# Hybrid decoder step with routed experts: the blocks of four experts moved behind the ranked pairs, and three edits ahead of them

## The chip, the cores and the metric

One core of a Trainium2 chip runs the whole step. The metric is the device time of one execution in microseconds (us); the median of three runs stands against the median of three runs of the changed kernel. One further execution was recorded by the profiler, and all rows below come from it.

## What is computed

A decoder layer is run on 288 tokens: 256 of a prompt and 32 of eight short samples. D is 2048, all in 32-bit floats.

```python
h  = rmsnorm(x, norm_mix)
y, conv, state = mixer(h)             # w_in, convolution + HGRN2 recurrence, w_out
x  = x + y
h2 = rmsnorm(x, norm_ffn)
ids, w = two_level_top2(h2)           # 4 groups of 8 experts; two experts per token
for e in range(32):                   # w_gate, w_up: 2048 x 512; w_down: 512 x 2048
    x += w[e] * (silu(h2 @ w_gate[e]) * (h2 @ w_up[e])) @ w_down[e]
out = rmsnorm(x, norm_final)
# outputs: the 288 rows, the new convolution buffers, the new recurrent states
```

The weights of an expert are 12.6 MB, those of all 32 are 403 MB, and each is read from HBM once.

## The kernel before

The kernel has one body, `trunk_step`. A planner orders each engine's instructions by priority on a simulated time line of its own; at run time every engine then takes its list strictly in order, and waits by semaphores. `tc.issue_after(i)` puts the instructions of its block that are on the engine of `i` behind `i` in that engine's list; it holds back no other engine.

**Front** (lines 250 to 336). `load_x` brings x in two halves. Seven short vectors are brought by GpSimd's queue into `prow`, transposed (line 280) and copied by ScalarE into `par` (line 281). The 16 column blocks of x are transposed by `xpose` (lines 291 to 294), eight per half of x. VectorE multiplies each with `par` and the norm's factor into `hT`, tiles `ha` and `hb` (line 316). The first two projections read `hT` and the raw weights (line 194); from the third on, `project` splits each weight tile on ScalarE into `hi` (line 201) and on VectorE into `lo` (line 202) and makes three matmuls per block (lines 205 to 207).

**Mixer and output projection** (to line 930). The mixer's columns follow, then 16 columns of `w_out`, with `raw`, `hi` and `lo` as weight slots. The recurrent states of sample heads 4 to 7 are finished here: `late_loads` (line 876) is called at column 2 and loads four 512 KB tiles into three of the five `xb` slots and scales them on VectorE behind each load (line 881); `late_state` (line 888) makes the update by four matmuls per head and half on TensorE, copies it on ScalarE and stores it by GpSimd's queue. Heads 4 and 5 are done behind the last column (line 930), heads 6 and 7 within the first pair of experts. Six of the first pair's gate tiles are loaded ahead (`load_ahead`).

**Routing** (lines 944 to 1050). VectorE computes the choice of experts; ScalarE makes `h2` in six pieces (line 963). `keys`, `weights` and `ids` compute the remaining places, the weights of the slots and the ranks of the later experts.

**Experts** (from line 1167). A `Block` has 128 rows: two experts of 64 rows, or four of 32. `gather` q (four quarters) brings the tokens by one-hot matmuls into `xg` (line 1180); `gu(vi, q)` makes a quarter of the gate (vi 0) or up (vi 1) product; `hidden` makes silu(gate) times up (lines 1209 and 1210), so its ScalarE instruction marks the time at which the gate product is done; `turn`, `down`, `out` and `combine` follow. All its matmuls go through `mm`, line 1062, in program order. The weights come in 1 MB tiles, 24 of them for a pair and 48 for a block of four, through a ring of 16 slots (`xa`, `xb`, `raw`, `hi`, `lo`) on SyncE's queue (line 867); a tile is asked for once its slot is free. `in_a_row` runs blocks so that the next block's gather lies beside the present one's down product. The last block ends in `last_down`, which takes the down weights by four column chunks (`wlast`, line 854), the last two of them in halves, and finishes the output norm.

The order of the blocks is: eight pairs of experts 0 to 15; then a block of four; a branch for overflow tiles, ahead of which ten tiles of the next block are loaded (`MIDPRE`); a second block of four; and four pairs. The four pairs hold the eight fullest of the experts 16 to 31, the blocks of four the eight others, by ranks computed on the chip and read into SyncE's registers (`static_id`).

## Time and profile before

| | us |
|---|---|
| median of three runs (lowest, highest) | 1599.75 (1597.68, 1601.33) |
| the profiled execution, its own time | 1599.1 |
| its span on the core | 1596.6 |
| TensorE busy (its granted clock, mean) | 1468.3 (0.971) |
| VectorE, ScalarE, GpSimd busy | 644.8, 448.2, 31.9 |
| moved by DMA | 492.78 MB |

Times in the rows are microseconds from the span's start. "L1062" is line 1062 of the kernel; behind `[` stands how long the engine had been idle ahead of the instruction, and what released it. A granted clock of 1.00 is 2.4 GHz, 0.50 is 1.2 GHz. Because `mm` is one helper, all expert matmuls have line 1062 and are told apart by their tiles: `tp` gather, `att` gate and up, `o` down, `z` combine.

### The profile page before, as it was taken

The page shows a single profiled execution, that of the slowest core. Times are in us where ns is not written, and L with a number is a line of the kernel's source. Part 1 is how long each engine was busy: PE and PEld are TensorE (multiplying, and loading weights), DVE is VectorE, ACT ScalarE, POOL GpSimd, SP SyncE. Part 2 cuts the span into 40 slices and gives each one's busy share as a digit, 9 for nine tenths or more (in the row PEclk, how much of TensorE's full clock was granted, in tenths as well). Part 3 has the DMA queues.
Part 4 walks back from the last instruction along what each step waited for, and adds up shares of the span by engine and source line. Part 5 has one row for each costly group of instructions (what it writes and reads, how often), then busy time and mean ns, then how long its engine had stood idle before and what let it go on. Part 6 is the DMA issues. An engine that isn't in the chain of part 4 may idle for free. (4 is left out here: it accounts for less than half of the span.)

```text
span 1596.6 us, 22199 instructions
## 1 busy us (share of the span) xinstructions
PE 1468.3 (92%) x8898; PEld 918.8 (58%) x8898; DVE 644.8 (40%) x1317; ACT 448.2 (28%) x968; POOL 31.9 (2%) x53
## 2 busy tenths in 40 slices
PE   5999999999979979999999999999666788999995
PEld 3999998999879954543544544544114242543531
DVE  4567788887554443223223223123013022313214
ACT  4467775985834451000000000000000000000013
POOL 1000001000000000000000000000000000000000
PEclk9999999999989989999999999999887899999998
DMA  9645446545498547999999999999998999999992
GB/s 218 172 117 155 138 140 189 159 137 135 111 255 253 156 158 287 396 408 416 419 411 417 419 414 417 419 415 420 418 408 359 421 406 421 415 415 421 415 405 94
DMA packets 228310, 492.78 MB, mean 309 GB/s; under 512 B 13593, under 2 KB 157545, under 8 KB 194936
## 3 DMA queue, kind: packets, MB, share of 16 engines
q1 hardware_dynamic: 225448, 485.09, 81.6%
q0 software_dynamic: 2608, 6.13, 1.2%
q8 instruction: 72, 1.18, 0.3%
q14 instruction: 38, 0.31, 0.1%
q10 hardware_dynamic: 144, 0.07, 0.0%
HBM read 483.92 MB, written 8.18 MB: 308 GB/s over the span
## 5 line engine op out<-in xcount | busy, mean ns | idle before, releaser
L1062 PE MATMUL att<-xb,xg 128*64 128x512 f32 (+1 forms) x640 | 175.2, 634 | 11.9 <-DMA xb<-in_w_exp_up_dram 9.6
L1062 PEld LDWEIGHTS tp<-P,h 96*128 96x128 f32 x1344 | 158.3, 196 | 42.8 <-issue 24.0
L1062 PE MATMUL tp<-P,h 96*128 96x128 f32 x1344 | 166.9, 283 | 15.1 <-DVE P L1169 8.6
L202 DVE TENSOR_TENSOR lo<-raw,hi 128x1024 fp32r<-128x1024 f32 x124 | 147.7, 1222 | 51.4 <-ACT hi L201 51.2
L201 ACT CAST hi<-raw 128x1024 fp32r<-128x1024 f32 x124 | 123.8, 1049 | 88.0 <-PE z L206 59.2
L1210 DVE TENSOR_TENSOR hid<-hid,att 128x512 f32<-128x512 f32 x14 | 9.6, 688 | 311.8 <-PE att L1062 311.8
L1062 PE MATMUL att<-raw,xg 128*64 128x512 f32 (+1 forms) x384 | 119.8, 617 | 8.5 <-DMA raw<-in_w_exp_up_dram 7.0
L1234 ACT ACTIVATE yh<-o,wc 128x512 fp32r<-128x512 f32 x56 | 38.5, 687 | 306.8 <-PE o L1062 287.5
L1062 PE MATMUL att<-xa,xg 128*64 128x512 f32 (+1 forms) x512 | 106.9, 618 | 10.2 <-DVE xg L1180 6.6
L1245 DVE TENSOR_TENSOR acc<-acc,z 96x512 f32<-96x512 f32 x104 | 66.6, 680 | 118.2 <-PE z L1062 118.0
L205 PE MATMUL z<-hhb,hi 128*128 128x288 f32 x368 | 112.0, 304 | 0.0
L206 PE MATMUL z<-hla,hi 128*128 128x288 f32 x368 | 110.9, 301 | 0.0
L207 PE MATMUL z<-hhb,lo 128*128 128x288 f32 x368 | 110.9, 301 | 0.0
L206 PE MATMUL z<-hlb,hi 128*128 128x288 f32 x368 | 110.6, 301 | 0.0
L205 PE MATMUL z<-hha,hi 128*128 128x288 f32 x368 | 110.2, 300 | 0.0
L207 PE MATMUL z<-hha,lo 128*128 128x288 f32 x368 | 109.8, 298 | 0.0
L1062 PE MATMUL att<-lo,xg 128*64 128x512 f32 (+1 forms) x256 | 101.2, 620 | 2.9 <-DMA lo<-in_w_exp_up_dram 2.9
L1235 DVE SCALAR_TENSOR_TENSOR yl<-o,wc,yh 128x512 fp32r<-128x512 f32 x56 | 41.9, 748 | 150.3 <-ACT yh L1234 148.7
L1062 PEld LDWEIGHTS att<-xb,xg 128*64 128x64 f32 (+1 forms) x640 | 49.1, 136 | 91.0 <-issue 69.8
L1180 DVE TENSOR_TENSOR xg<-tp,npm 128x512 f32<-128x512 f32 x56 | 38.7, 692 | 141.6 <-PE tp L1062 141.5
L1062 PE MATMUL att<-hi,xg 128*64 128x512 f32 (+1 forms) x256 | 89.8, 597 | 5.7 <-DMA hi<-in_w_exp_up_dram 5.7
L1218 ACT COPY hd<-tp 128x512 f32<-128x512 f32 x14 | 8.2, 585 | 306.9 <-PE tp L1062 306.9
(433 smaller groups left out, 2569.4 us busy)
## 6 DMA issues: line engine op xcount, KB each, us to landing
raw<-in_w_in_dram SPq DMA_DIRECT2D x48, 1024.0 KB, 5.8
xb<-in_w_exp_gate_dram SPq DMA_DIRECT2D x40, 1024.0 KB, 17.8
xb<-in_w_exp_up_dram SPq DMA_DIRECT2D x40, 1024.0 KB, 12.2
xb<-in_w_exp_down_dram SPq DMA_DIRECT2D x40, 1024.0 KB, 13.3
xa<-in_w_exp_gate_dram SPq DMA_DIRECT2D x32, 1024.0 KB, 15.6
xa<-in_w_exp_down_dram SPq DMA_DIRECT2D x32, 1024.0 KB, 11.9
xa<-in_w_exp_up_dram SPq DMA_DIRECT2D x32, 1024.0 KB, 13.5
raw<-in_w_exp_gate_dram SPq DMA_DIRECT2D x24, 1024.0 KB, 17.1
```

The costliest lines, as they stand in the source:

```text
L201: S.copy(wh[:, ks], w[:, ks])
L202: V.tensor_sub(wl[:, ks], w[:, ks], wh[:, ks].bitcast(F32))
L205: T.matmul(ps[:, :N], wh[:, k], xh[k], start=i == 0, stop=False)
L206: T.matmul(ps[:, :N], wh[:, k], xl[k], start=False, stop=False)
L207: T.matmul(ps[:, :N], wl[:, k], xh[k], start=False, stop=i == KT - 1)
L1062: i = f(*args, **kw)
L1180: V.tensor_mul(self.xg[:, 4 * q:4 * q + 4], pb, npm[:, 4 * q:4 * q + 4, None].to_broadcast([128, 4, 128]))
L1210: V.tensor_mul(self.hid, self.hid, self.pg[1])
L1218: S.copy(self.hd, pb)
L1234: S.activation(yh, py, AF.Copy, scale=self.wc[:, 2:3])
L1235: V.scalar_tensor_tensor(yl, py, self.wc[:, 2:3], yh.bitcast(F32), op0=ALU.mult, op1=ALU.subtract)
L1245: V.tensor_add(av, av, ps[t][:TT])
```

## The change

- The four ranked pairs run directly behind the eight pairs; then the first block of four, the branch, and the second block of four, which is now the last block and ends in `last_down`. `wlast` takes any number of experts.
- In the first pair the steps go gate 0, up 0, gate 1, up 1 and so on, not all of gate and then all of up; the tiles loaded ahead follow that order.
- The scaling of the late states is taken out of `late_loads` and done at column 7. Heads 6 and 7 are finished behind the routing's `sel` matmuls on TensorE and behind the first half of `h2` on ScalarE; the second half of `h2` stands behind them on ScalarE.
- `keys` stands behind the multiply of gather 0 on VectorE (before: behind the one-hot), `weights` and `ids` behind that of gather 1 and, on ScalarE, behind `h2`. The transposes of the slot rows are a function of their own, behind the fourth step of the first pair.
- The transposes of x's second half stand behind that of the parameters on TensorE; `par` is copied by VectorE.
- The PSUM banks of the output projection and of the experts are one layout: `y` becomes `att`, the logits' `gsm` becomes `o`, and no pool is closed in between.

```diff
-PS2 = dict(y=2, tp=2, o=1, gsm=1)
...
-    T.transpose(pb[:, :NPAR], prow, ident[:NPAR, :NPAR])
-    S.copy(par, pb[:, :NPAR])
+    par_t = T.transpose(pb[:, :NPAR], prow, ident[:NPAR, :NPAR])
+    V.tensor_copy(par, pb[:, :NPAR])
...
-    for k in range(8, KT):
-        xpose(k, S.copy)
+    with tc.issue_after(par_t.ins):
+        for k in range(8, KT):
+            xpose(k, S.copy)
...
-    banks(**PS2)
+    banks(**PS3)
...
-    prl = bank("gsm")
+    prl = bank("o")
...
-    def wlast(e0, e1, q, cuts):
+    def wlast(es, q, cuts):
-        ws = [xslot().rearrange("p (k c) -> p k c", c=512) for _ in range(2)]
+        ws = [xslot().rearrange("p (k c) -> p k c", c=512) for _ in es]
...
+    def late_scale():
+        for hh in range(4):
             V.tensor_mul(ls0[hh // 2][:, hh % 2], ls0[hh // 2][:, hh % 2],
...
+    def late_state(hh, tag):
+        st = ls0[hh // 2][:, hh % 2]
+        for u in range(2):
+            su = st[:, 4 * u:4 * u + 4]
+            pn = bank(tag)
+            T.matmul(pn, lkm[:, hh], lvx[:, 4 * u:4 * u + 4], start=True, stop=False)
+            T.matmul(pn, ident, su, start=False, stop=True)
+            i = S.copy(su, pn.rearrange("p (b v) -> p b v", v=128))
+        G.dma_start(out=o["new_hgrn_sample"][0, :, 4 + hh].rearrange("b d v -> d b v"), in_=st)
+        return i
...
+        if es is None:
+            which, q, e = i // 2 % 2, i // 4, i % 2
...
-            ps = project(w_out, c, chi, clo, tag="zzyy"[c % 4])
+            ps = project(w_out, c, chi, clo, tag=("z", "z", "att", "att")[c % 4])
...
+        if c == 7:
+            late_scale()
...
-    late_state((0, 1), T.matmul)
+    for hh in range(2):
+        late_state(hh, "z")
...
-    for u in range(2):
+    def h2_half(u):
...
+    i = h2_half(0)
+    with tc.issue_after(i.ins), tc.issue_after(sel.ins):
+        late_state(2, "att")
+        i = late_state(3, "z")
+    with tc.issue_after(i.ins):
+        h2_last = h2_half(1)
...
+            steps = [(vi, q) for vi in range(2) for q in range(4)]
+            if n == 0 and first:
+                steps = [(vi, q) for q in range(4) for vi in range(2)]
+            for i, (vi, q) in enumerate(steps):
+                p.gu(vi, q)
+                if n == 0 and vi == 0 and q < 3:
+                    g1 = p.gather(q + 1)
+                    if first and q == 0:
+                        with tc.issue_after(g0.ins):
+                            k = keys()
+                        with tc.issue_after(g1.ins), tc.issue_after(h2_last.ins):
+                            wts = weights()
+                            ids(*k)
...
+                if i == 3:
...
+                    if first and n == 0:
+                        slot_rows(wts)
                     p.slots()
...
-    in_a_row(blocks + [Later(lambda: quad(0))], first=True)
+    pairs = [Later(lambda i=i: Block([ranked_id(2 * i + u) for u in range(2)], NST * CAP + 128 * i))
+             for i in range(NDP)]
+    in_a_row(blocks + pairs + [Later(lambda: quad(0))], first=True)
     q1 = quad(1)
...
-    in_a_row([q1] + [Later(lambda i=i: Block([static_id(2 * i + u) for u in range(2)], NST * CAP + 128 * i))
-                     for i in range(NDP)], last=True)
+    in_a_row([q1], last=True)
```

## Rows read from the trace of the kernel before

**Rows 1.** page of the profile, section 2: GB/s moved in 40 slices of the span

```profile
GB/s 218 172 117 155 138 140 189 159 137 135 111 255 253 156 158 287 396 408 416 419 411 417 419 414 417 419 415 420 418 408 359 421 406 421 415 415 421 415 405 94
```

**Rows 2.** busy time by stretch: stretch, length, then PE, PEld, DVE, ACT, POOL; PEclk, DMA share, GB/s

```profile
1120.00:1160.00 40.00, 26.26 (x130) 6.04 (x132) 0.69 (x1) 0.58 (x1) 0.00 (x0) 0.87 1.02 418
```

**Rows 3.** ACT timeline, 600 to 1600: start, length, line, operation; idle before and releaser

```profile
634.09 0.60 ACT L1209 ACTIVATE hid<-att 128x512 f32<-128x512 f32 x1 [12.12 <-PE att L1062]
1057.53 0.60 ACT L1209 ACTIVATE hid<-att 128x512 f32<-128x512 f32 x1 [16.88 <-PE att L1062]
1118.05 0.60 ACT L1209 ACTIVATE hid<-att 128x512 f32<-128x512 f32 x1 [16.91 <-PE att L1062]
1530.87 0.60 ACT L1209 ACTIVATE hid<-att 128x512 f32<-128x512 f32 x1 [16.88 <-PE att L1062]
```

**Rows 4.** chain of work that ended last: start, length, what

```profile
1300.45 18.46 DMA hi<-in_w_exp_down_dram
1574.77 3.61 PE o L1062 x16
```

**Rows 5.** busy time by stretch, as in rows 2: the branch and the end

```profile
1215.00:1220.00 5.00, 4.17 (x23) 3.87 (x26) 2.22 (x8) 0.00 (x0) 0.00 (x0) 0.50 0.13 56
1540.00:1545.00 5.00, 5.00 (x10) 1.21 (x10) 0.00 (x0) 1.32 (x3) 0.00 (x0) 0.62 1.05 388
1555.00:1560.00 5.00, 4.10 (x17) 1.18 (x17) 0.61 (x1) 0.69 (x1) 0.00 (x0) 1.00 0.95 350
```

**Rows 6.** PE timeline, 1180 to 1300, a block of four waiting for weights

```profile
1183.60 1.06 PE L1062 MATMUL o<-hi,hd 128*32 128x512 f32 x1 [1.51 <-DMA hi<-in_w_exp_down_dram]
1290.53 3.64 PE L1062 MATMUL o<-xa,hd 128*32 128x512 f32 x32
```

**Rows 7.** timeline of all engines, the first 50 us

```profile
4.40 0.48 POOL L268 DMA_DIRECT2D prow<-in_hgrn_norm_g_dram  x1
18.19 4.05 PE L293 MATMUL tp<-ident,xt 96*128 96x96 f32 x24
25.55 1.99 ACT L201 CAST hi<-raw 128x1024 fp32r<-128x1024 f32 x2 [2.87 <-DMA raw<-in_w_in_dram]
27.44 0.21 ACT L281 COPY par<-gsm 128x73 f32<-128x73 f32 x1
28.90 3.52 DVE L316 SCALAR_TENSOR_TENSOR ha<-xa,par,rb 128x288 f32<-128x288 f32 x8
29.47 2.29 PE L194 MATMUL z<-ha,raw 128*128 128x288 f32 x4 [7.11 <-DVE ha L316]
48.83 0.40 PE L205 MATMUL z<-hhb,hi 128*128 128x288 f32 x1
```

**Rows 8.** DMA issues of the first 45 us: issue, count, size, median us to landing

```profile
prow<-in_hgrn_norm_g_dram POOLq DMA_DIRECT2D x1, 0.5 KB, 8.0
```

**Rows 9.** timelines of DVE and of PE, 450 to 475

```profile
464.79 1.23 DVE L881 TENSOR_TENSOR xb<-xb,gsd 128x1024 f32<-128x1024 f32 x1 [4.44 <-DMA xb<-in_state_hgrn_dram]
467.66 0.61 PE L207 MATMUL y<-chh,lo 128*128 128x288 f32 x1 [5.15 <-DVE lo L202]
```

**Rows 10.** timelines of DVE and of PE, 590 to 650, routing and first pair

```profile
594.10 0.16 DVE L1031 TENSOR_REDUCE pt<-ge 96x3 f32<-96x12 f32 x1 [5.39 <-ACT ge L1025]
598.69 0.65 DVE L1180 TENSOR_TENSOR xg<-tp,npm 128x512 f32<-128x512 f32 x1
599.40 5.19 PE L1062 MATMUL att<-xa,xg 128*64 128x512 f32 x16 [6.60 <-DVE xg L1180]
610.64 1.02 PE L1062 MATMUL z<-xb,ident 128*128 128x512 f32 x2
623.05 3.65 PE L1062 MATMUL att<-xb,xg 128*64 128x512 f32 x16 [0.78 <-DVE xg L1180]
647.68 5.63 PE L1062 MATMUL tp<-P,h 96*128 96x128 f32 x48
```

**Rows 11.** busy time by stretch, as in rows 2: the routing

```profile
580.00:585.00 5.00, 1.84 (x5) 0.66 (x5) 3.90 (x18) 4.36 (x5) 0.00 (x0) 1.00 0.25 93
```

More of the change, by code (lines that the diff above doesn't have):

```diff
@@ L886, in late_loads, with load_ahead @@
                      C("hm2")[:, :, None].to_broadcast([128, 4, 128]))
-    def late_state(heads, mul):
-        for hh in heads:
-            st = ls0[hh // 2][:, hh % 2]
-            for u in range(2):
-                su = st[:, 4 * u:4 * u + 4]
-                pn = bank("z")
-                mul(pn, lkm[:, hh], lvx[:, 4 * u:4 * u + 4], start=True, stop=False)
-                mul(pn, ident, su, start=False, stop=True)
-                S.copy(su, pn.rearrange("p (b v) -> p b v", v=128))
-            G.dma_start(out=o["new_hgrn_sample"][0, :, 4 + hh].rearrange("b d v -> d b v"), in_=st)
-    ahead = {}
-    def load_ahead(i, es=(0, 1)):
-        n = len(es)
-        which, q, e = i // (4 * n), i % (4 * n) // n, es[i % n]
+    def late_state(hh, tag):
[8 more added lines that the diff above has]
+        return i
+    ahead = {}
+    def load_ahead(i, es=None):
+        if es is None:
+            which, q, e = i // 2 % 2, i // 4, i % 2
+        else:
+            n = len(es)
+            which, q, e = i // (4 * n), i % (4 * n) // n, es[i % n]
         ahead[which, who(e), q] = wload(which, e, q)
@@ L950, in trunk_step @@
     for t in range(NT):
-        T.matmul(tp[:TT, t * 36:(t + 1) * 36], xlg[:, t * TT:(t + 1) * TT], C("sel"), start=True, stop=True)
+        sel = T.matmul(tp[:TT, t * 36:(t + 1) * 36], xlg[:, t * TT:(t + 1) * TT], C("sel"), start=True, stop=True)
     for t in range(NT):
@@ L1285, in in_a_row @@
             if n == 0:
-                pi = p.onehot()
-                p.gather(0)
-            for vi in range(2):
-                for q in range(4):
-                    mi = p.gu(vi, q)
-                    if n == 0 and vi == 0:
-                        if first and q == 0:
-                            late_state((2, 3), mm)
-                        if q < 3:
-                            p.gather(q + 1)
-                        if first and q == 0:
-                            with tc.issue_after(pi.ins), tc.issue_after(mi.ins):
-                                k = keys()
-                                weights()
-                                ids(*k)
-                    if prev is not None and vi == 0 and q < 2:
-                        prev.out(2 + q, py[q])
-                        prev.combine(2 + q, CT)
-                if vi == 0:
+                p.onehot()
+                g0 = p.gather(0)
+            steps = [(vi, q) for vi in range(2) for q in range(4)]
[11 more added lines that the diff above has]
+                            ids(*k)
+                if prev is not None and i < 2:
+                    prev.out(2 + i, py[i])
+                    prev.combine(2 + i, CT)
+                if i == 3:
                     if nxt is not None:
@@ L1330, in last_down @@
         for c in range(4):
-            ws = wlast(*p.e, c, CUTS if c >= CUT0 else 1)
+            ws = wlast(p.e, c, CUTS if c >= CUT0 else 1)
             py = bank("o")
@@ L1403, in quad @@
     def quad(i):
[L1404 removed]
+        return Block([ranked_id(2 * NDP + 4 * i + u) for u in range(4)], b0 + 128 * i)
     class Later:
```

20 lines of the change are left out of this document (10 added, 10 removed).

## The prediction

> **What bounds the kernel now.** I read four views. The page's transfer line first [rows 1]: up to slice 15 the core moves 110 to 290 GB/s, from slice 17 on about 415. So two stages with different limits: mixer and routing, and from about 600 us on the experts, whose 403 MB hardly let the queue rest. Then the ScalarE time line, in which one silu per block marks the time when its gate product is done [rows 3]. From 634.09 to 1057.53 lie seven pairs: 60.49 us each. A pair is 25.17 MB, so 416 GB/s. The list of TensorE's waits shows no wait for a transfer in these pairs, so TensorE paces them and the 16 slots are always full of its next tiles. A block of four has twice the bytes for the same matmuls: there TensorE is busy 26.26 of 40 us, and the transfers run at 418 GB/s [rows 2]. So pairs are paced by TensorE, blocks of four by the transfers.
>
> Third, the chain that ended last and the stretches at the end: the last weights land at about 1558 (350 GB/s in 1555 to 1560, and 94 in the page's last slice) [rows 1, 5], but the span ends at 1596.6. The kernel ends with pairs, so TensorE still has work in its slots while the queue is already empty. That is 38 us in which the resource that limits the sum of all blocks does nothing. Fourth, the time lines of the places that the other edits touch.
>
> **The order of the blocks (about -12 us).** I follow the same marks. In the kernel before, the gate of the first block of four is done at 1118.05 [rows 3], and the last down tile of the second one lands at 1300.45 + 18.46 = 1318.91 [rows 4]: 200.9 us, the branch's hole included (56 GB/s in 1215 to 1220) [rows 5]. With four more pairs ahead, at 60.49 us each, 242.0 us, the same landing falls at 1560.9, if nothing else changes. The ranked pairs cost no more than the fixed ones: they ended with the mark at 1530.87 [rows 3] and their tiles come at the same rate [rows 1]. Their ids are read on SyncE ahead of the loads; they are computed in the routing, hundreds of us earlier.
>
> What is behind that landing? The last block now takes its sixteen down tiles by column chunks. The eight such tiles of the kernel before went at 388 GB/s [rows 5], the rest near 420 [rows 1]: 16.8 MB x (1/388 - 1/420) = 3.3 us more. When the last half tile lands, 10 of a chunk's 32 matmuls are left: 3.64 us per 32 at full clock, twice that at half clock [rows 6], so an estimate of 1.1 to 2.2 us; I take 2.2. From the end of the last `o` group, 1574.77 + 3.61 = 1578.38 [rows 4], to the end of the span are 18.2 us, and these stay. Sum: 1560.9 + 3.3 + 2.2 + 18.2 = 1584.6 against 1596.6, 12.0 us. Bounds: 15.3 if the column tiles are as fast as the others, 6 by the clock rival below.
>
> **The parameters (about -6 us).** The first projection waited 7.11 us, until 29.47, for `ha` [rows 7]. `ha` needs `par`; ScalarE copied it at 27.44, because its list had two casts of a weight tile ahead of it, and that tile landed only at 25.55 [rows 7]. Yet the last of the seven vectors was issued at 4.40 and took 8.0 us [rows 7, 8]: it lay there at 12.4. The new order makes TensorE wait for it ahead of x's last 24 transposes, which began at 18.19 [rows 7]; 12.4 is earlier, so this wait costs nothing (if the landing came after 18.2, all 24 transposes and the first projection would queue behind it). VectorE can then make `ha` right behind the norm's factor. TensorE is free at 18.19 + 4.05 = 22.2, and 29.47 - 22.2 = 7.2 us can go; up to 2 more if the 19.4 us between 29.47 and the third projection at 48.83 [rows 7] also close up. It can be nothing: if VectorE's list keeps the `lo` splits ahead of `ha`, these wait for the same tile. I take 6, since the second half of x is still copied on ScalarE beside those casts.
>
> **The late states at the output projection (about -4 us).** At column 2 VectorE stood 4.44 us waiting for a state tile; the `lo` split that TensorE needed was queued behind it, and TensorE lost 5.15 us [rows 9]. At column 7 the tiles have long landed. Upper bound 7: the 5.15 and about 2 for matmuls at a lower clock after the pause. Lower bound 0: what is late next are the raw tiles of the following columns, which share the queue with the states and the tiles ahead (255 and 253 GB/s, the two fullest slices before 600 us but one) [rows 1]. I take 4.
>
> **The routing (about -6 us).** The first gate matmuls waited 6.60 us for the multiply of gather 0 [rows 10]. TensorE was done with that gather at 599.40 - 6.60 = 592.8, but VectorE ran the multiply at 598.69, as its list had `weights` ahead, and that waited 5.39 us for an exponential that stood on ScalarE behind all six pieces of `h2` [rows 10]. Now `keys` and `weights` stand behind the multiply. The other pairs wait 0.78 us there (623.05) [rows 10], so the gate starts at about 593.6, 5.8 us earlier.
>
> Against this stand the 16 matmuls of heads 6 and 7, now ahead of it. In the first pair they ran from 604.59 (599.40 + 5.19) to 611.66 [rows 10], 7.1 us. TensorE worked 1.84 of 5 us in 580 to 585 [rows 11], so some 3 us there are free, and more up to the one-hot. Worst case they all stand ahead of gather 0: 5.8 - 7.1 = -1.3; best case TensorE keeps its clock and the first group takes 3.65 and not 5.19 us [rows 10]: 7.3. I take 5.8. Their four copies and two stores go with them. Behind them on ScalarE now stands the second half of `h2`, some 2 to 4 us later; gather 2 needs it, three steps of 3.65 us after the gate's start, so that is the cover. `weights` and the slot rows come behind it, with over 20 us until the fourth step.
>
> **The first pair (about -7 us).** From the gate's start to the end of its up product it took 647.68 - 599.40 = 48.3 us [rows 10]. The 7.1 us of late states leave it. The waits of 0.78 us at three gathers can hide behind the up steps, at most 2.3; the slot rows' twelve transposes now stand in one place and wait for their own banks, so I book no gain for that. Bounds 4 and 9.4. Its tiles: 13 of 16 are asked for before the routing, the last three go into the `xb` slots of the late states, which now come free in the routing and not in the pair. If the stores held them until 620, the third step's successors would still be ahead of them.
>
> **Sum.** 12.0 + 6 + 4 + 5.8 + 7.1 = 34.9: span 1561.7. Around the span of the profiled execution lie 1599.1 - 1596.6 = 2.5 us, and the median is 0.65 above that execution: 1564.5 after rounding down a little. Is the queue fast enough for it? 371 of 384 tiles of 1.0486 MB remain at the routing's end; at 417 GB/s 933 us. From about 583 that gives 1516, with the hole and the column tiles about 1524, while TensorE's pace needs the last one at 1541. So TensorE paces, and nothing of the five terms is lost to the queue.
>
> **Rivals.** (1) The clock at the end. In a block of four TensorE waits for each tile, and its granted clock is 0.87 [rows 2], with matmuls of 1.06 us in the bad stretches [rows 6]. At half clock a chunk takes 7 us of `o`, 1.5 of the two copies and 3 of combine, 11.6 against 10.8 us of transfers: TensorE is late by 0.8 us per chunk and by about 3 in the last. Then the order brings 6, not 12: 1570.5. For it: the last block never has work stored up. Against: the fast groups of 3.64 us in the second block of four [rows 6]. The Trainium skill, TensorE: Matmul & The Clock Gate, section HAM oscillation, states that matmul bursts with waits for the next slice between them start at the slow clock again and again, which speaks against ending on such blocks; by it the result is this rival's, and the row of 1.06 us agrees for one stretch, the row of 3.64 us does not.
>
> (2) The front edits don't do what they say: the planner's new lists put another wait in place of the two removed, and terms two and three are 0: 1574.5. For it: the plan is made on simulated times, and put the parameters' transpose last though its data lay there. Against: TensorE has 5 to 7 us of plain idle time at both places.
>
> (3) Slower: the transfers fall below TensorE's pace in the pairs. They need 416 GB/s and the best slice of the page is 421 [rows 1], so there is 1% to spare. At the 388 of the column tiles [rows 5] a pair would take 64.9 us, twelve pairs 53 us more, and the result would be 18 us slower, 1617. It decides from 34.9 / 12 = 2.9 us per pair, that is 397 GB/s. Against: the ranked pairs already ran at 415 to 420 [rows 1] with the same tiles.
>
> (4) The lead of the queue grows: it starts 12 us earlier, and the blocks of four find more landed: up to 10 us better, about 1553.
>
> **How the numbers follow.** Forecast 0.55, clock 0.18, front 0.14, slower 0.04, queue's lead 0.06, no gain because a wait in routing or at the branch eats it (near 1600) 0.03. Most likely 1564. All bounds together would be 1551 to 1590; they won't all fall to one side, and I end at 1584. A change of 0.2%, 3.2 us, is about what can be told from none: faster 0.93, same 0.03, slower 0.04.
>
> **What would show it.** Right: silu marks 60.5 us apart for twelve pairs, the first near 1350 for the block of four being 25 us below 1118 + 242; the end of the last landing about 20 us ahead of the span's end; first projection near 23; no 5 us wait at column 2; the gate starting 0.8 us behind gather 0. Wrong: waits for `xb` or `raw` tiles in the pairs, a granted clock of 0.5 over the last 20 us, or the two halves of `h2` on the chain.

## The result and the profile after

| | us |
|---|---|
| the changed kernel, median (lowest, highest) | 1575.85 (1574.84, 1576.59) |
| the kernel before, beside it | 1599.56 (1597.68, 1601.33) |
| ratio, 95% interval | 0.9851 (0.9834, 0.9869) |
| forecast, range | 1564.0 (1551 to 1584) |
| the changed kernel's profiled execution, its span | 1576.59, 1574.8 |

The change makes the kernel 23.7 us faster. The sign was right and the time lies in the range, but 12 us above the forecast. 1575.85 is next to rival 2, whose time was 1574.5. The spans of the two profiled executions differ by 21.8 us; the rest lies around the spans (2.5 us before, 1.8 after) and in the distance of the profiled executions from the medians.

The program was profiled a second time, beside the last experiments: median 1576.83, span 1574.8 again, but with another sum inside it. I cut each span at two marks, the first matmul of the gate and the end of the first pair's up product (the 48 gather matmuls behind it); of before these are 599.40 and 647.68 [rows 10].

| stretch | forecast | first profile | second profile |
|---|---|---|---|
| start to the gate (front -6, output projection -4, routing -5.8) | -15.8 | -3.3 | -0.4 |
| gate to the end of the first pair's up product | -7.1 | -9.8 | -9.8 |
| from there to the end of the span (order of the blocks) | -12.0 | -8.7 | -11.6 |
| sum | -34.9 | -21.8 | -21.8 |

Here is what the table is read from. The time line of TensorE at the two marks, in the changed kernel, first profile (start, length, line, operation, count, then the idle time before it and what ended it):

```profile
589.11 1.13 PE L896 MATMUL z<-xb 128*128 128x512 f32 x2 [1.98 <-ACT xb L898]
...
592.33 2.94 PE L1081 MATMUL tp<-P,h 96*128 96x128 f32 x24 [0.77 <-DVE P L1181]
596.06 3.65 PE L1081 MATMUL att<-xa,xg 128*64 128x512 f32 x16 [0.79 <-DVE xg L1199]
...
634.55 5.62 PE L1081 MATMUL tp<-P,h 96*128 96x128 f32 x48
```

ScalarE's marks of the blocks, as in [rows 3]: the last two pairs and the first block of four. The pairs are 60.5 us apart as before:

```profile
1225.94 0.60 ACT L1228 ACTIVATE hid<-att 128x512 f32<-128x512 f32 x1 [16.88 <-PE att L1081]
1286.44 0.60 ACT L1228 ACTIVATE hid<-att 128x512 f32<-128x512 f32 x1 [16.88 <-PE att L1081]
1347.04 0.60 ACT L1228 ACTIVATE hid<-att 128x512 f32<-128x512 f32 x1 [16.99 <-PE att L1081]
```

Busy time by stretch (columns as in [rows 2]), the branch and the end, which answer to [rows 5]:

```profile
1440.00:1445.00 5.00, 3.13 (x13) 2.87 (x14) 3.36 (x15) 0.00 (x0) 0.00 (x0) 0.50 0.73 295
1445.00:1450.00 5.00, 4.17 (x20) 2.86 (x24) 0.69 (x1) 0.00 (x0) 0.00 (x0) 0.50 0.20 85
1450.00:1455.00 5.00, 5.00 (x38) 2.09 (x31) 0.00 (x0) 0.00 (x0) 0.00 (x0) 0.79 0.65 221
1455.00:1460.00 5.00, 4.22 (x41) 2.42 (x43) 0.69 (x1) 0.00 (x0) 0.00 (x0) 1.00 0.96 324
...
1540.00:1545.00 5.00, 4.56 (x31) 1.09 (x24) 2.41 (x5) 1.45 (x6) 0.00 (x0) 1.00 1.05 386
```

And TensorE at the last tile:

```profile
1521.02 3.62 PE L1081 MATMUL o<-xa,hd 128*32 128x512 f32 x26 [1.66 <-DMA xa<-in_w_exp_down_dram]
...
1554.45 0.62 PE L1081 MATMUL o<-hi,hd 128*32 128x512 f32 x1 [0.23 <-DMA hi<-in_w_exp_down_dram]
```

The last tile is there at 1554.45, 20.4 us ahead of the end; in the kernel before these were 38. The granted clock is 1.00 in 1540 to 1545, as in the other stretches from 1515 to 1560 of this profile. The page's transfer line, which answers to [rows 1], shows 414 to 422 GB/s over the pairs:

```profile
GB/s 220 172 112 153 136 159 162 170 146 151 96 214 292 157 174 301 422 415 416 420 415 417 419 414 418 418 415 418 417 414 420 416 415 421 421 409 328 418 396 222
```

The front, time lines of DVE, ACT and PE, which answer to [rows 7]:

```profile
25.89 1.99 ACT L200 CAST hi<-raw 128x1024 fp32r<-128x1024 f32 x2 [8.51 <-DMA raw<-in_w_in_dram]
...
26.96 1.23 DVE L201 TENSOR_TENSOR lo<-raw,hi 128x1024 fp32r<-128x1024 f32 x1 [7.71 <-ACT hi L200]
28.10 0.23 DVE L280 COPY par<-gsm 128x73 f32<-128x73 f32 x1
28.25 1.22 DVE L201 TENSOR_TENSOR lo<-raw,hi 128x1024 fp32r<-128x1024 f32 x1
29.38 3.51 DVE L316 SCALAR_TENSOR_TENSOR ha<-xa,par,rb 128x288 f32<-128x288 f32 x8
...
28.23 1.70 PE L292 MATMUL tp<-ident,xt 96*128 96x96 f32 x9 [6.95 <-ACT xb L293]
29.95 2.29 PE L193 MATMUL z<-ha,raw 128*128 128x288 f32 x4
48.77 0.40 PE L204 MATMUL z<-hhb,hi 128*128 128x288 f32 x1 [1.18 <-ACT sg L536]
```

The copy of `par` moved to VectorE, but there it stands between the two `lo` splits, and these wait 7.71 us for ScalarE's cast, which waits 8.51 us for the weight tile. The first projection starts at 29.95 (before 29.47), the third at 48.77 (before 48.83): nothing gained. ScalarE's copies of x stand behind the same cast, so TensorE's transposes wait 6.95 us as well.

The output projection, DVE and PE, which answer to [rows 9]:

```profile
465.28 1.23 DVE L884 TENSOR_TENSOR xb<-xb,gsd 128x1024 f32<-128x1024 f32 x1 [5.93 <-DMA xb<-in_state_hgrn_dram]
468.16 0.61 PE L206 MATMUL att<-chh,lo 128*128 128x288 f32 x1 [6.64 <-DVE lo L201]
```

The multiplies are called at column 7 in the source, yet they stand at column 2 in VectorE's list as before, with a wait of 5.93 us (before 4.44) and TensorE behind it 6.64 us (before 5.15). The last logits' matmuls start at 576.85 (before 576.71; second profile 578.12).

The routing, ScalarE and TensorE, beside the wait of 1.98 us at 589.11 above:

```profile
581.42 6.22 ACT L973 ACTIVATE h<-acc,rs 96x1024 f32<-96x1024 f32 x3 [0.61 <-DVE rs L178]
588.48 1.05 ACT L898 COPY xb<-z 128x512 f32<-128x512 f32 x2
...
590.93 0.18 PE L1027 MATMUL o<-mb,trib 96*96 96x32 bf16 x1
```

ScalarE makes the first half of `h2` until 587.64 and only then copies the late states' products (line 898). TensorE waits for one of these copies until 589.11, makes the last product, and reaches the ranks' matmuls (line 1027) at 590.93, though VectorE had their input ready at 585.7.

### The profile page after: what moved, and what is told of

Its sections match the earlier page's. It is cut to its first block, busy times and chain, and to the rows that moved or that the text cites. A ratio compares the mean times of both kernels' runs of the same rounds, so it can differ in the third digit from the quotient of the medians.

```text
span 1574.8 us, 22207 instructions
## 1 busy us (share of the span) xinstructions
PE 1458.2 (93%) x8898; PEld 911.6 (58%) x8898; DVE 645.7 (41%) x1318; ACT 446.2 (28%) x967; POOL 31.8 (2%) x53
## 5 line engine op out<-in xcount | busy, mean ns | idle before, releaser
L1081 PE MATMUL att<-xb,xg 128*64 128x512 f32 (+1 forms) x640 | 168.2, 613 | 7.2 <-DMA xb<-in_w_exp_up_dram 5.7
L1081 PE MATMUL att<-lo,xg 128*64 128x512 f32 (+1 forms) x256 | 111.8, 615 | 4.3 <-DMA lo<-in_w_exp_up_dram 4.3
L1081 PE MATMUL att<-hi,xg 128*64 128x512 f32 (+1 forms) x256 | 105.2, 625 | 1.4 <-DMA hi<-in_w_exp_up_dram 1.4
L428 ACT ACTIVATE pd<-ep,wdw 128x256 f32<-128x256 f32 x216 | 91.5, 502 | 0.1
## 6 DMA issues: line engine op xcount, KB each, us to landing
xa<-in_w_exp_up_dram SPq DMA_DIRECT2D x34, 1024.0 KB, 13.8
```

Of the source, the lines that this page charges most:

```text
L428: S.activation(pg[:, i], ep[:, w:w + NP], AF.Identity, scale=wdw[:, j, w:w + 1], bias=bdw[:, j:j + 1] if w == 0 else 0.0)
L1081: i = f(*args, **kw)
```

## The experiments

Lines in the short diffs are against the kernel that each expectation names. A time of a run is its median; a ratio is to the kernel before, measured beside it; a stretch is from its profile, which is one execution. The experiments stand on three chips, and the kernel before took 1602.67 us beside the first four, 1598.76 and 1598.75 beside the others, so across chips the ratios are the fairer measure. The changed kernel's ratios are 0.9851 (0.9834 to 0.9869) and, measured again, 0.9857 (0.9842 to 0.9872). Where a run's interval overlaps these, its effect on the whole time is not clear of noise, and only the stretches carry the reading.

**One half at a time.** First the new order of the blocks without the rest, on the kernel before:

```diff
-    in_a_row(blocks + [Later(lambda: quad(0))], first=True)
+    in_a_row(blocks + pairs + [Later(lambda: quad(0))], first=True)
...
-    in_a_row([q1] + [Later(lambda i=i: Block([static_id(2 * i + u) for u in range(2)], NST * CAP + 128 * i))
-                     for i in range(NDP)], last=True)
+    in_a_row([q1], last=True)
```

> The kernel before, with the new order of the blocks alone: quad 0, the twelve pairs, then the last block of four (its down tiles by column chunks, as the second block had them). Routing, first pair and front are those of before. My theory: the order's gain stands by itself, about 8.7 us (12.0 forecast, less what the hole at the branch and the column tiles took in the changed kernel), so 1591 us, ratio 0.9945, and the last landing to the end of the span is near 20 us. Rival: the order pays only because the routing starts the experts earlier (the queue has its lead from there); then this kernel is within 3 us of before, 1597 to 1600. Second rival: the forecast of 12 was right and the other edits of the changed kernel take 3 us back at the branch; then 1588.

1587.63 against 1602.67 for the kernel before beside it, ratio 0.9911 (0.9892 to 0.9930). In the profile the first pair's up product ends at 649.30, and from there to the end of the span of 1587.8 it is 938.5 us against 948.9 in before: 10.4 us.

```profile
649.30 5.62 PE L1062 MATMUL tp<-P,h 96*128 96x128 f32 x48
```

The order stands by itself. By the stretch its size is between my 8.7 and the forecast's 12; by the ratio the kernel is 14 us faster (11 to 17), and my 0.9945 lies outside the interval. The second rival's 1588 was nearest in time, but its reason (the other edits take 3 us back at the branch) is not borne out: the changed kernel's second profile, with all edits, has 11.6 us in this stretch. This run also serves as a second profile of the old routing and first pair: from the last logits to the gate it is 22.7 us and the pair takes 48.4, as in before.

Then the rest without the order, in the changed kernel:

```diff
-    in_a_row(blocks + pairs + [Later(lambda: quad(0))], first=True)
+    in_a_row(blocks + [Later(lambda: quad(0))], first=True)
...
-    in_a_row([q1], last=True)
+    in_a_row([q1] + pairs, last=True)
```

> The changed kernel with the old order of the blocks (quad 0, second block of four, then the pairs) and all other edits as they are. My theory: routing 3.3 us and first pair 9.8 us earlier, front and output projection nothing: 13 us below before, 1586.5, ratio 0.992; the gate starts near 596 us, gu ends 38.5 us later, and the whole shift arrives at the end, because TensorE and not the queue paces the pairs. Rival: part of the 13 us is lost to the queue at the two blocks of four, which are paced by transfers (they would start from the same queue); then 1590 to 1596. With the first experiment: the two gains should add up to about 22 to 24 us; if they add up to less, the order needs the rest.

1589.13, ratio 0.9926 (0.9906 to 0.9947), by the ratio 11.9 us below before.

```profile
633.93 5.62 PE L1081 MATMUL tp<-P,h 96*128 96x128 f32 x48
```

The first pair's up product ends 13.8 us earlier than in before, and the last stretch is 948.9 us as in before (span 1582.8), so in this profile, the fastest of its executions, all was won ahead. Both ratios times each other give 0.9838, and the changed kernel has 0.9851: within the intervals the two halves add up and do not need each other.

**The front.** x's copies and `ha`, `hb` ahead of the first casts and splits, as the forecast had assumed them to be; the chain of `lt` ahead as well:

```diff
-        with tc.high_priority(LOPRI):
+        with tc.high_priority(LOPRI), ExitStack() as es_:
+            for i in hold:
+                es_.enter_context(tc.issue_after(i))
...
+    hold += [xlast.ins, hlast.ins]
...
+    with tc.high_priority(LOPRI):
         V.tensor_max(lt[:, 0], lbl[:, 0:8], lbl[:, 8:16])
```

> The changed kernel with VectorE's and ScalarE's lists in the front put as the forecast assumed them: the first hi casts and lo splits stand behind x's last copy and behind ha and hb. The forecast's theory: TensorE's wait of 7 us for ha goes, the first projection starts near 23 us instead of 30, and up to 6 us arrive at the end: 1570, ratio 0.996 against the changed kernel. Rival, which I now hold likelier: another chain is late at the same place (the weight tile that lands at 25.5, its hi casts and lo splits now behind ha, then the third projection, which waits for the activation of its group): the first projection may start 1 to 3 us earlier and the third stays at 48 to 49 us: 1574 to 1576, no change, or 1 to 3 us later, if the splits that now come later are needed first.

1571.12, ratio 0.9812 (0.9796 to 0.9828): 4.7 and 5.7 us below the changed kernel's two medians, 6 to 7 us by the ratios. Time lines of DVE and PE in this run:

```profile
18.80 0.23 DVE L283 COPY par<-gsm 128x73 f32<-128x73 f32 x1
19.15 1.37 DVE L319 SCALAR_TENSOR_TENSOR ha<-xa,par,rb 128x288 f32<-128x288 f32 x3
21.19 2.58 PE L193 MATMUL z<-ha,raw 128*128 128x288 f32 x8
...
31.89 2.12 PE L193 MATMUL z<-hb,raw 128*128 128x288 f32 x4 [2.16 <-DVE hb L319]
...
43.37 0.40 PE L207 MATMUL z<-hhb,hi 128*128 128x288 f32 x1 [0.19 <-ACT sg L541]
```

`par` is there at 18.80 and `ha` starts at 19.15, where the changed kernel had them at 28.10 and 29.38. The first projection starts at 21.19. A new wait appears at 31.89, because VectorE stood 6.23 us at the router's weights ahead of `hb`; the third projection comes at 43.37, 5.4 us earlier than in the changed kernel. The last logits come at 572.86, 4.0 and 5.3 us earlier than in the changed kernel's two profiles. So the forecast's 6 was about the right size for what it described, and the change did not do it; how much of it the earlier chain of `lt` gave was not tried apart. My own expectation, that another chain would take all of it, was wrong.

**The scaling of the late states.** Really behind column 7's copy:

```diff
-        V.tensor_copy(xc, ps)
+        xci = V.tensor_copy(xc, ps)
...
-            late_scale()
+            with tc.issue_after(xci.ins):
+                late_scale()
```

> The changed kernel with the four multiplies of the late states really behind column 7's copy of the output projection; in the changed kernel the call stood there, but the planner put them in VectorE's list at column 2, where the wait of 5.93 us for the state tile still is. The forecast's theory: TensorE's wait of 6.64 us at column 2 goes and about 4 us arrive at the routing's gate and at the end: 1572, ratio 0.9975 against the changed kernel; bounds 0 and 7. Rival: the raw tile of the same column lands no earlier, so a wait for the raw tile or its hi cast stands at the same place; then 0 to 1 us.

1577.53, ratio 0.9847 (0.9827 to 0.9867): no gain that can be told from none. Column 2's copy comes at 473.58, 2.94 us earlier, and the last logits at 575.84, only 1.0 us earlier than in the first profile of the changed kernel (2.3 earlier than in the second): two columns behind the four multiplies TensorE waits 1.68 us for a cast, and the columns there take 2 us longer. The routing then loses more than that:

```profile
588.11 1.39 PE L896 MATMUL z<-xb 128*128 128x512 f32 x2 [1.99 <-ACT xb L898]
592.70 5.49 PE L1082 MATMUL tp<-P,h 96*128 96x128 f32 x24 [0.67 <-DVE P L1182]
598.97 5.38 PE L1082 MATMUL att<-xa,xg 128*64 128x512 f32 x16 [0.78 <-DVE xg L1200]
```

Gather 0 takes 5.49 us here and 2.94 in the changed kernel; the granted clock is 0.50 from 590 to 600. Both expectations missed this; the wait at column 2 did go. That the fall of the clock belongs to this edit is not shown: in the second profile of the changed kernel, below, the clock falls at the same pause without it.

One multiply each behind columns 6, 8, 10 and 12:

```diff
-        if c == 7:
-            late_scale()
+        if c in (6, 8, 10, 12):
+            with tc.issue_after(xci.ins):
+                late_scale(c // 2 - 3)
```

> The changed kernel with the four multiplies of the late states one by one behind the copies of columns 6, 8, 10 and 12 of the output projection. All four behind column 7 won 2.94 us at column 2 and gave 1.9 back at columns 7 and 8, where TensorE waited behind them. My theory: one multiply of 1.23 us per two columns lies beside TensorE's 7.2 to 7.5 us per column, so the 2.9 us reach the last column's copy and the gate: 1573, ratio 0.998. Rival: what comes off here the routing takes back (gather 0 at half clock after the longer pause, as with all four behind column 7): gate within 1 us of 596 or later, 1575 to 1578.

1569.08, ratio 0.9808 (0.9795 to 0.9821): 7.7 us below the changed kernel beside it, much more than I expected, and mostly for another reason. The last logits come at 576.57, 1.5 us earlier than in the second profile of the changed kernel. But one product of the late states now has its slot in TensorE's list as early as 556.7, within a column, so that the routing has one less:

```profile
586.70 0.18 PE L1030 MATMUL o<-mb,trib 96*96 96x32 bf16 x1
591.94 3.65 PE L1084 MATMUL att<-xa,xg 128*64 128x512 f32 x16 [0.83 <-ACT h L976]
```

The ranks' matmuls follow the other products directly at 586.70 (changed kernel 590.93), without the wait for a copy, and the gate starts at 591.94 instead of 596.06 or 599.04. From the last logits to the gate it is 15.4 us, against 19.2 and 20.9. This is read from the time line; no run moved that product alone.

**The routing and the first pair.** The late states of heads 6 and 7 back in the first pair:

```diff
-    with tc.issue_after(i.ins), tc.issue_after(sel.ins):
-        late_state(2, "att")
-        i = late_state(3, "z")
...
             p.gu(vi, q)
+            if first and i == 0 and n == 0:
+                late_state(2, "z", mm)
+                late_state(3, "z", mm)
```

The two halves of `h2` then follow each other on ScalarE, as in the kernel before.

> The changed kernel with the late states of heads 6 and 7 back in the first pair, behind its first step. In the changed kernel they run from 580.0 to 591.9 in the routing; the last of them waits 1.98 us for a copy on ScalarE, and the ranks' matmuls, whose input lay there from about 585.7, stand behind it: VectorE's key waits 5.53 us. My theory: without them the gate starts 5 us earlier, near 591, and the pair takes 7.1 us longer, 45.6: together 2 us later than the changed kernel, 1578. So of the forecast's 7.1 us for the move about 2 remain, and the rest of the pair's gain pays back what they cost in the routing. Forecast's theory (they lie beside other work in the routing): the gate starts no earlier than 595, and the kernel is 7 us later, 1583.

1578.88, ratio 0.9876 (0.9859 to 0.9894).

```profile
586.31 0.19 PE L1023 MATMUL o<-mb,trib 96*96 96x32 bf16 x1 [3.82 <-DVE mb L1014]
588.06 4.75 PE L1077 MATMUL tp<-P,h 96*128 96x128 f32 x24 [0.76 <-ACT h L973]
593.60 3.65 PE L1077 MATMUL att<-xa,xg 128*64 128x512 f32 x16 [0.78 <-DVE xg L1195]
...
638.95 5.62 PE L1077 MATMUL tp<-P,h 96*128 96x128 f32 x48
```

The ranks run at 586.31 and not at 590.93, and would give a gate near 591.7, but gather 0 runs at half clock (4.75 us). The pair takes 45.35 us, 6.9 more than the 38.49 of the changed kernel. So the late states are off the pair at their full price, as forecast. In the routing, where the ranks stand behind them, they cost part of it again: from the last logits (577.36) to the gate it is 16.2 us here, against 19.2 and 20.9 in the changed kernel, so 3.0 and 4.7 us, although the clock fell here. My expected 1578 came; the forecast's theory, that they lie beside other work in the routing, did not.

The ranks ahead of the last of them:

```diff
-        i = late_state(3, "z")
+        late_state(3, "z", us=(0,))
...
+    with tc.issue_after(rk.ins):
+        i = late_state(3, "z", us=(1,))
     with tc.issue_after(i.ins):
         h2_last = h2_half(1)
```

> The changed kernel with the last two products of the late states (second half of head 7) behind the ranks' matmuls instead of ahead of them, and the second half of h2 behind those as before. In the changed kernel the ranks' input lay there at 585.7, TensorE was free of the other late states at 587.1, waited 1.98 us for a copy, did the last ones, and reached the ranks only at 590.93. My theory: the ranks run at 587.1, gather 0 at about 589 behind key and the last products, the gate starts 2 to 3 us earlier, near 593.5, and the kernel is at 1573.3, ratio 0.9985 against the changed one. Rival: the last products, now between the ranks and gather 0, still wait for the copy that stands behind half of h2 on ScalarE (until 589.1), and gather 0 behind them: gate at 595, gain at most 1 us; or TensorE's clock falls in the pause and eats it.

1575.21, ratio 0.9842 (0.9827 to 0.9856), 1.6 us below the changed kernel beside it, with overlapping intervals. The ranks ran at 587.99, but the last products still waited 1.52 us for ScalarE's copy, until 590.13, and then went ahead of gather 0 at half clock (1.82 and 1.91 us for two matmuls each); the gate started at 597.27.

```profile
590.13 1.82 PE L896 MATMUL z<-xb 128*128 128x512 f32 x2 [1.52 <-ACT xb L898]
```

That is the rival: the copy stays in the way, and the clock falls in the pause.

The keys and weights ahead of gather 0's multiply again (`pi` is the one-hot, `mi` the last matmul of the step):

```diff
-                        with tc.issue_after(g0.ins):
+                        with tc.issue_after(pi.ins), tc.issue_after(mi.ins):
                             k = keys()
-                        with tc.issue_after(g1.ins), tc.issue_after(h2_last.ins):
```

> The changed kernel with keys, weights and ids where they stood before, ahead of the multiply of gather 0 on VectorE. My theory: the wait of 6.60 us that the kernel before had at its gate comes back almost whole, since the exponential still stands on ScalarE behind half of h2 and the late states' copies: gate near 601 instead of 596.06, kernel 1580, ratio 1.003 against the changed one. Rival: in the changed kernel the late states delay the ranks so much that the exponential is done by then; the gate moves by less than 2 us, 1577.

1578.32, ratio 0.9867 (0.9850 to 0.9884). The gate comes at 601.10, as expected, and its first group at half clock:

```profile
600.28 0.16 DVE L1049 TENSOR_REDUCE pt<-ge 96x3 f32<-96x12 f32 x1 [2.35 <-ACT ge L1043]
601.10 6.67 PE L1081 MATMUL att<-xa,xg 128*64 128x512 f32 x16 [3.37 <-DVE xg L1199]
```

The multiply again stands behind the exponential (2.35 us of wait) and the rest of `weights`, TensorE waits 3.37 us, and its first sixteen matmuls take 6.67 us instead of 3.65. From the last logits (577.60) to the gate it is 23.5 us, against 19.2 and 20.9 in the two profiles of the changed kernel: the place of the keys is worth 2.6 to 4.3 us. The lower figure compares like with like, as in the second profile the matmuls ahead of the ranks ran at half clock, and so they did here (1.85 and 1.91 us for two). The half clock of the first group took 3 more in this execution. At the end 1.5 to 2.5 us are seen, with overlapping intervals.

The first pair in the old order of its steps:

```diff
-            if n == 0 and first:
-                steps = [(vi, q) for q in range(4) for vi in range(2)]
```

> The changed kernel with the first pair's steps back in the old order, the four quarters of gate and then the four of up (the loads ahead asked for in the same order). In the changed kernel the gate starts at 596.06 and the up product ends at 634.55, 38.5 us. My theory: the mixed order is worth what the waits for the gathers' multiplies were worth, three times 0.78 us, so the pair takes 40.8 us, and the kernel 1578, ratio 1.0015 against the changed one. Rival: the mixed order is worth nothing, because the whole gain of the pair (9.8 us against the forecast 7.1) is the late states' 7.1 us and the places of keys and slot rows; then 38.5 us and 1576. Second rival: with the old order the slot rows are late in the fourth step; then 44 us or more.

1577.53, ratio 0.9864 (0.9847 to 0.9880). From the gate at 596.36 to 637.55 it is 41.2 us, 2.7 more than in the changed kernel; the waits of 0.78 us ahead of the three later gathers' groups are back. My expectation of 2.3 us for the mix was about right; the kernel's end shows 1 to 2 of them, with overlapping intervals.

**The branch.**

```diff
-MIDPRE = 10
+MIDPRE = 11
```

> The changed kernel with eleven instead of ten tiles of the last block asked for ahead of the branch. In the changed kernel the queue falls to 43 GB/s for 5 us at the branch (1447 to 1452), and some 7 us of transfer are lost there. My theory: the queue runs dry because the tiles ahead are too few for the time from the last of them to the first ask behind the branch; one more tile of 1.05 MB is 2.5 us less of hole, and as transfers pace the last block, the kernel is 2.5 us earlier: 1573.4. Rival: the eleventh tile has no free slot until the branch is through (its request waits on the queue, and the branch behind it): no gain, or a loss of 1 to 3 us.

1575.33, ratio 0.9853 (0.9836 to 0.9870): no gain. Waits of SyncE's queue around the branch, and the stretches of the hole:

```profile
SPq L1454 <- SPq L1454: 20.5, 6, 5.1
1445.00:1450.00 5.00, 4.00 (x20) 3.09 (x24) 0.69 (x1) 0.00 (x0) 0.00 (x0) 0.50 0.47 198
1450.00:1455.00 5.00, 5.00 (x38) 1.77 (x29) 0.00 (x0) 0.00 (x0) 0.00 (x0) 0.78 0.12 33
1429.27 2.82 SPq L867 DMA_DIRECT2D xb<-in_w_exp_gate_dram  x2
1453.67 1.57 SPq L867 DMA_DIRECT2D raw<-in_w_exp_gate_dram  x3
```

SyncE's queue stands 20.5 us at the branch (line 1454), in this run and in the first profile of the changed kernel alike; in its second profile and in the kernel before it is 18.9 us, and over all runs 18.4 to 20.6. What it waits for there the profile does not name. The tenth and eleventh tile are issued from 1429.27 over 2.82 us, so the eleventh at about 1431.8, when its slot is free, and the first one behind the branch at 1453.67: 21.9 us. In the changed kernel the tenth and last is issued at 1429.04 and the first behind the branch at 1450.86: 21.8 us (second profile 1432.03 and 1452.27: 20.2 us). The branch starts one tile later and ends one tile later. Against a steady 418 GB/s the stretches 1440 to 1460 (370, 198, 33, 390) lack 8.1 us of transfer, between the 8.9 and 7.2 of the changed kernel's two profiles, which are worked out below. The hole only moves; the rival was right that nothing is gained.

**All three repairs together**: the front's order, the spread multiplies, the ranks first.

> The front's order of the splits, the spread multiplies and the ranks ahead of the last late states together, on the changed kernel. Theory: the gains add up, 4 to 6 of the front, 2.9 and 2 to 3 us, as all lie one behind the other on the way to the gate: about 1567 for this kernel, ratio 0.9935 against the changed one. Rival: the routing's start is late to something else (the state tiles, the raw tiles of the last columns, the clock of gather 0), so that only the largest arrives: 1570 to 1572.

1564.30 (1563.50 to 1565.50), ratio to before 0.9783 (0.9769 to 0.9796), 12.5 us below the changed kernel beside it; this is the fastest version here.

```profile
581.43 0.18 PE L1034 MATMUL o<-mb,trib 96*96 96x32 bf16 x1 [0.40 <-DVE mb L1025]
...
587.38 3.65 PE L1092 MATMUL att<-xa,xg 128*64 128x512 f32 x16 [0.83 <-ACT h L982]
...
625.87 5.62 PE L1092 MATMUL tp<-P,h 96*128 96x128 f32 x48
```

The last logits come at 572.46 (second profile of the changed kernel: 578.12), the ranks wait only 0.40 us for VectorE's choice, and the gate starts at 587.38 instead of 599.04: 5.7 us from ahead of the routing and 6.0 in it (against the first profile 4.4 and 4.3). The pair still takes 38.49 us. Taken singly the three repairs gave 5 to 6, 7.7 and 1.6 us, 14 to 15 in sum; together it is 12.5, so most of each arrives, and 1564.30 is 3 us better than my 1567. In this run too a product of the late states has moved into a column, at 552.6. That the time equals the forecast's 1564 is chance: it is the sum of other terms than the forecast's and proves none of them.

**The changed kernel once more**, beside these:

> The changed kernel unaltered, beside the three others on the same chip, as the measure for them and for the spread from execution to execution: ratio to the kernel before 0.985, 1574 to 1578. What it settles: the last block's time from its first mark to its last product was 209.3 us in the first profile and 205.5 to 208.4 in kernels that do not differ there; if this execution gives 205 to 207, the first one had a large hole at the branch by chance, and the order's gain is 10 to 12 us rather than 8.7.

1576.83, ratio 0.9857 (0.9842 to 0.9872). From the first block of four's mark (1350.01) to the last product of the last block it is 206.3 us, not 209.3. In this execution the order gives 11.6 us, and the routing gives less than in the first:

```profile
590.00:595.00 5.00, 4.15 (x15) 1.87 (x15) 0.46 (x2) 1.71 (x4) 1.02 (x2) 0.66 0.59 164
590.39 2.04 PE L896 MATMUL z<-xb 128*128 128x512 f32 x2 [1.99 <-ACT xb L898]
599.04 3.65 PE L1081 MATMUL att<-xa,xg 128*64 128x512 f32 x16 [0.78 <-DVE xg L1199]
...
637.53 4.73 PE L1081 MATMUL tp<-P,h 96*128 96x128 f32 x40
```

(The view ends at 642, within the last group.) The wait ahead of the last late states' product is the same 1.99 us as the 1.98 of the first profile, but two matmuls then take 2.04 us instead of 1.13.

## Why the prediction was right or wrong, step by step

**What bounds the kernel** was right: twelve pairs at 60.5 us each, paced by TensorE, a block of four paced by the transfers; the rival with transfers below TensorE's pace did not come (414 to 422 GB/s over the pairs).

**The order of the blocks (12.0)** was right in mechanism and nearly in size. The first profile shows 8.7, the others that have the new order 9.9 to 12.5, by the same stretch against 948.9 of before. The term carried over "the branch's hole included" from the kernel before, and there lies what is short in the first profile: the hole is not the same in every execution. Against a steady 418 GB/s, the four stretches 1440 to 1460 of the changed kernel lack (4 x 418 - 295 - 85 - 221 - 324) / 418 x 5 = 8.9 us; the same for before, 1210 to 1225 (357, 56 [rows 5] and 364 GB/s), gives 5.7. In the second profile it is 7.2 (383, 175, 90, 418). The 1.7 us between the two profiles go with the time that SyncE stood at the branch, 20.5 and 18.9 us; that it was 18.9 in before too, with a hole of 5.7, shows that this is not all of it. The mark forecast "near 1350" stands at 1347.04, but that is no hit: the forecast's own sum, 1360 less 22.9 for the terms ahead, gives 1337, and the mark is late by the 10 us that those terms gave less.

The rival of the half clock came in part, and its price did not. In the first profile the groups of the last down product ran at full clock: the 26 matmuls behind a wait of 1.66 us took 3.62 us. But in the up product of the same block the granted clock was 0.69 in 1490 to 1495 and 0.67 in 1500 to 1505, behind waits of 1.43 and 1.44 us, and in the second profile it fell in the down product too, to 0.75 in 1530 to 1535:

```profile
1532.57 1.06 PE L1081 MATMUL o<-lo,hd 128*32 128x512 f32 x1 [1.59 <-DMA lo<-in_w_exp_down_dram]
```

There the last tile's matmul still starts at 1554.40, against 1554.45 in the first profile, 20.4 us ahead of the end in both: TensorE then waited for the transfers again, and what the clock had cost did not reach the end. The Trainium skill, TensorE: Matmul & The Clock Gate, section HAM oscillation, describes bursts of matmuls that each start at the slow clock after a wait for the next slice; its example has longer waits than the 1.67 us here, some groups of this block agree with it and others do not, and the forecast's use of it as a price for the end was not borne out. Nor did the queue's lead grow: in the run with all repairs the experts start 11.7 us earlier than in the second profile of the changed kernel, and their stretch to the end is 937.2 us against 937.3.

**The parameters (6)** failed at the step "VectorE can then make `ha` right behind the norm's factor". The forecast named the condition itself ("it can be nothing: if VectorE's list keeps the `lo` splits ahead of `ha`"), and took 6 of 7.2 all the same. The trace of before had the reason against it: ScalarE's list already put a cast that waited until 25.55 ahead of `par`, whose data lay there [rows 7]. A planner that does this on one engine can do it on the other. The run with the order forced gave 5 to 6 us by the medians: the size was right, the condition was not met. Measured in the changed kernel, the term was nothing.

**The late states at the output projection (4)** failed twice. The step "at column 7 the tiles have long landed" took the place of a call for the place in a list; the multiplies stayed at column 2. And the size was too large: with the multiplies really moved, column 2 gave 2.9 us, of which between 0.3 and 2.3 were left at the last logits, depending on which run and which profile of the changed kernel are compared. That spreading them was at the same time worth 3.8 or 5.5 us in the routing, with one product now within a column, nothing in the forecast saw.

**The routing (5.8)** gave 3.5 in the first profile and 1.8 in the second, from the last logits to the gate (22.7 us before, 19.2 and 20.9 after). The wait for the exponential went, as forecast, and the keys' place is worth 2.6 to 4.3 us. The step that failed is where the late states were put beside other work: the sum's value counted them as free, with -1.3 as the bound. They end behind the ranks' input, at 590.9 against 585.7, because the last one waits for a copy that ScalarE makes only behind half of `h2`. Back in the pair they left the routing 3.0 to 4.7 us shorter. So the prediction's last sign of being wrong, the halves of `h2` on the chain, came true for the first half. The bounds of -1.3 and 7.3 held; the value of 5.8 stood too near the good one.

**The first pair (7.1)** gave 9.8: the late states 6.9 as forecast, and the mixed order 2.7, for which I had "at most 2.3" and booked nothing. Both together lie a little above the upper bound of 9.4.

**Rivals.** The second had the right content (terms two and three are nothing), with a chance of 0.14 against 0.55 for the sum. Its time, 1.4 us from the measured one, is in part luck: it left the other three terms as they were, and of these the order and the routing gave less, the first pair more. Its sentence "the plan is made on simulated times" was the one to follow. Moreover the sum took 6 (of 0 to 9.2) for the parameters and 5.8 (of -1.3 to 7.3) for the routing, both near the good bound and both resting on a list's order, so they could fail together. The sum itself is 1564.85 by its own terms; it was put at 1564.

What stays open: why the granted clock falls at the pause of 2 us in one execution and not in the next, why SyncE stands 18.4 us at the branch in one and 20.6 in another, and why a later gate (in the run with the keys ahead by 5 us against the first profile, by 2 against the second) shows only in part at the end: the last stretch, with the hole at the branch in it, was shorter there (936.4 us).

## What to carry to other kernels

When an edit works by moving a call, and a planner orders the lists, read the new list before counting the gain: an operation with data from a late transfer ahead of the one that was to be freed makes the edit worth nothing. Price the moved work at its new place by what is queued behind it there, not by the engine's idle share. And a tail in which the queue is empty while the compute engine still has stored work is worth reordering: here it gave 8.7 and 11.6 of the 21.8 us between the spans, with no work saved.

## What the runs showed of the hardware

- TensorE's granted clock at a short pause differs between executions of one program. After some 7 us of matmuls without a gap, and a wait of 1.98 to 1.99 us, the next two took 1.13 us in one execution and 2.04 in another (granted 1.00 and 0.66 in 590 to 595); the gate's start differs by 3.0 us, of which 1.3 were there already at the last logits. Eight of the profiles here have this same wait: in four the two matmuls behind it took 1.12 or 1.13 us, in the four others 1.39, 1.85, 1.96 and 2.04.
- A branch held SyncE's queue for 18.4 to 20.6 us, with ten tiles or eleven asked for ahead of it; the transfers ran dry behind the tiles in flight, at 33 to 90 GB/s in the emptiest of the 5 us stretches above (the kernel before had 56 [rows 5]).
- Down tiles by column chunks ran at 383 to 389 GB/s, as in [rows 5], with the DMA engines fully busy, while the pairs' tiles went at 414 to 422.
